# A gated feed-forward layer on one Trainium2 core: one pair of up-projection groups per layer computed token-major, with seven-product blocks

## The chip, the cores and the metric

The kernel runs on one core of one Trainium2 chip. The metric is the device time in microseconds of one execution. The engines are TensorE (PE, with its weight loads as PEld), VectorE (DVE), ScalarE (ACT), GpSimd (POOL) and SyncE (SP); SP and POOL issue the DMAs here.

## The reference

Two layers over 256 positions of width 2048, all in fp32. Layer 0 mixes positions with a gated MLP over blocks of 128, layer 1 with latent attention; each mixer is followed by a gated MLP with a causal width-3 convolution, which is what the change touches:

```
D_MODEL = 2048; SEQ = 256; DEPTH = 2; D_FF = 5504

def conv_ffn(x, w_up, conv_w, conv_b, w_down):
    h = x @ w_up                                    # (256, 2048) @ (2048, 11008)
    h = causal_depthwise_conv(h, conv_w) + conv_b   # width 3, along positions
    a, g = jnp.split(h, 2, axis=-1)
    return (jax.nn.silu(g) * a) @ w_down

x = layer_norm(ALPHA * x + mixer(x));  x = layer_norm(ALPHA * x + conv_ffn(x, ...))
```

## The kernel before

Every fp32 product is made of three products of rounded parts: high by high, low by high, high by low. A weight therefore has to be split: ACT casts its high part and DVE subtracts it to get the low part.

**The stream of weights.** All weights pass through one list of chunks of 1 MB (`Feed`, from line 73 on). SP loads a chunk into one of 3 "raw" slots, ACT and DVE split it (`wh` L127, `wl` L130) into two of 14 "big" slots, and the products read those. Splits are issued two chunks ahead of the use in the program; a scheduler then lays out the order on each engine, keeping each queue in order at run time. Chunk numbers stand in the names: `wl178` is the low part of chunk 178.

**Two forms of product.** In the feature-major form (`prod_a`) the weight block stands in the array and the activations stream: per group of 256 columns of the gate half and 256 of the value half, four chunks, four PSUM banks, 64 matmuls of 128x512 and 64 of 128x256. The result has features on partitions, as the convolution wants it. In the token-major form (`Banks`) the activation block stands and the weights stream, always 128x512; eight chunks serve four direct banks (`q3`, `p2`, `e`, `q4`) by `eight` with 24 matmuls a chunk. For a chunk marked "seven", `Feed._seven` (L133 on) also forms sums of the chunk's four 128x512 blocks (`ts`, then `th` and `tl`), and `Banks.seven` takes 21 matmuls in place of 24, using four more banks (`p1`, `q5`, `p7`, `p6`) and sums of the activations (`turn`, `combine`). `Banks.rest` (L448 on) combines the four extra banks on DVE. The token-major form with seven-chunks is used in the phases called v, u, wo, mo and dn.

**Up and down.** `ffn` runs up for groups 1 to 21 of four chunks each (group 0 is done earlier, with the mixer's end), all feature-major, seven-products nowhere. After each group `pair` runs twice: an ACT copy `lo` and a DVE sum `h` (L388, L390) join the halves of two banks, then the convolution (ACT L909, DVE L910 and L912), `silu` (ACT L926) and the product `act` (DVE L927). The names carry the pair's number: `h_0a15` is layer 0, value half, pair 15, that is, group 7. `act` tiles hold eight pairs each; from the fifth on (`act0_4`, `act0_5`) they live in "side" slots. Down (`dn`) follows, token-major in two halves, with every third or so chunk a "seven"; its banks take over those of the last up groups as the `h` rows free them.

**Parking.** Eight of the down chunks are split ahead, during up, and stored: `Feed.park` loads one by POOL (`praw`), splits it (`pwh`, `pwl`), makes the sums (four adds, L154) and splits those (`pth`, `ptl`); POOL stores the four results to DRAM (`keptwh`, `keptwl`, `keptth`, `kepttl`) and later fetches them (`fwh`, `fwl`, `fth`, `ftl`, L189). Six "side" slots hold all this. A chunk takes four steps, a layer 32; each step is taken by `next(jobs)` after chunks 1 and 2 of a group, from group 2 on. In layer 0 the parked chunks are 231 (used second in down), 236, 241 and so on to 266, the last that is parked. POOL's queue is in order, so a fetch that waits holds the ones behind it.

Of the kernel before, what the change touches and what calls it, by code (L numbers as in the profile page):

```python
# [8 lines left out]
F32 = mybir.dt.float32  # L9
# [6 lines left out]
P = 128  # L16
S = 256
# [35 lines left out]
U_SEVEN = [(2, 3)] + [(2, 3, 4)] * 4 + [(2, 3)]  # L53

MO_SEVEN = (1, 2)

T1, T2 = 6, 5
SLOTS = {"big": 14, "raw": 3, "side": 6}
# [15 lines left out]
def plan(n_k):  # L74

    return [[(int(t[:-1]), KINDS[t[-1]]) for t in line.split()] for line in PLAN[n_k]]
# [135 lines left out]
def trunk(ctx: ExitStack, tc: tile.TileContext, x, xT, gm_in, gm_wout, ffn_up, ffn_dn,  # L212
# [12 lines left out]
    def slot(shape, name, dt=F32, tag="big"):  # L225
        return big.tile(shape, dt, tag=tag, name=name, bufs=SLOTS[tag])

    def bank(name):
        return ps.tile([P, 512], F32, tag="bank", name=name)
# [27 lines left out]
    def back(w, n_k):  # L257

        for hf, units in enumerate(plan(n_k)):
            c = slice(hf * 1024, (hf + 1) * 1024)  # L260
            for u, kind in units:
                if 2 * u + 1 == n_k:
                    chunks.append((w[2 * u, :, c], 1024, kind))
                    continue
                if kind == "parked":
                    parked.append(len(chunks))
                chunks.append((w[2 * u : 2 * u + 2, :, c].rearrange("k p c -> p k c"), 2048, kind))

    back(gm_wout, NF_GM)
    chunks += [(ffn_up[0, i], 2048, "") for i in range(n_up)]  # L270
    back(ffn_dn[0], NF_FF)
    chunks += [(ml_q[i], 2048, "") for i in range(4)]
    chunks += [(ml_kv[i], 3 * KVR, "") for i in range(5)] + [(ml_kv[5, :, 0:KVR], KVR, "")]
    chunks += [(ml_b[i], 2048, "") for i in range(ml_b.shape[0])]
    chunks += [(ml_out[i], 2048, "seven" if i - 8 in MO_SEVEN else "") for i in range(ml_out.shape[0])]
    chunks += [(ffn_up[1, i], 2048, "") for i in range(n_up)]
    back(ffn_dn[1], NF_FF)


# [18 lines left out]
    def combine(name, o, k1, k2):  # L298


        t = tp.tile([P, 4, P], F32, tag="t2", name=f"xs{name}", bufs=T2)
        turn(t, k1, k2)
        o = o.rearrange("p (h s c) -> p h s c", h=2, s=4)
        nc.scalar.copy(o[:, 0], t)
        nc.vector.tensor_tensor(o[:, 1], t, o[:, 0].bitcast(F32), ALU.subtract)
        return [(o[:, 0, i], o[:, 1, i]) for i in (1, 2, 0, 3)]
# [556 lines left out]
    def park_all(until):  # L863

        for i in [i for i in parked if feed.used < i < until]:
            yield from feed.park(i)
            yield
# [48 lines left out]
    def ffn(layer, ln, acc, end, last):  # L916
        act = [None] * 6
        acts = Acts(act, f"dn{layer}", NF_FF)

        def pair(a, acc_a, acc_g):  # L920
            if act[a // 8] is None:
                act[a // 8] = slot([P, 8, S], f"act{layer}_{a // 8}", tag="side" if a // 8 > 3 else "big")
            ca = conv(layer, a, acc_a, f"{layer}a{a}")
            cg = conv(layer, NF_FF + a, acc_g, f"{layer}g{a}")
            s = tp.tile([P, S], F32, tag="t1", name=f"s{layer}_{a}", bufs=T1)
            nc.scalar.activation(s, cg, AF.Silu)  # L926
            nc.vector.tensor_tensor(act[a // 8][:, a % 8, :], s, ca, ALU.mult)  # L927

        hb, ht = [], [None, None]

        def after(b, step, acc):
            if step == 0:
                ht[b] = tp.tile([P, 512], F32, tag="t2", name=f"upt{layer}_{b}", bufs=T2)
                nc.scalar.copy(ht[b], acc)
                return
            if b == 0:
                hb.extend(bank(f"uph{layer}_{f}") for f in range(2))
            for f in range(4):
                o = (f % 2) * S + b * P
                nc.tensor.transpose(hb[f // 2][:, o : o + P], ht[b][:, f * P : (f + 1) * P], ident)  # L940

        boundary(ln, acc, end, f"upf{layer}_", after)
        xhl, old = ln.new, ln
        jobs = park_all(feed.used + 2 * n_up)
        for gi in range(1, 22):
            nt, nk = (4, 4) if gi < 21 else (2, 8)
            acc = [bank(f"up{layer}_{gi}_{f}") for f in range(nt)]
            for c in range(KD // nk):
                hi, lo = feed.next()
                prod_a(acc, xhl, range(nk * c, nk * c + nk), hi, lo)  # L950
                if gi > 1 and c in (1, 2) and gi + c > 3:
                    next(jobs, None)
                if (gi, c) in FIRST:
                    acts.make(*plan(NF_FF)[0][FIRST.index((gi, c))])
                if gi == 1 and c == 0:
                    after(1, 1, None)
                    for f in range(2):
                        pair(f, hb[0][:, f * S : (f + 1) * S], hb[1][:, f * S : (f + 1) * S])
            for f in range(nt // 2):
                pair(2 * gi + f, acc[f], acc[nt // 2 + f])  # L960
            if 1 < gi < 6:
                old.restore(gi - 2)
            if gi in (4, 6):
                old.park(gi // 2 - 2)
        ln = Norm(2 * layer + 1, {}, old.put_away, last)
        return (ln, *down(NF_FF, act, f"dn{layer}", ln, acts, 4 if last else SKEW))
# [406 lines left out]
```

## Time and profile before

| | |
|---|---|
| median of 3 runs | 2464.81 us (2464.58 to 2466.5) |
| the profiled execution's own time | 2465.45 us |
| its span | 2463.7 us |
| granted TensorE clock | 1.000 |
| DMA | 611.94 MB, mean 248 GB/s |

The span is what the profiler saw from the first to the last instruction. In the rows shown below, busy times are microseconds; "x" counts instructions; a group's row gives busy time and mean nanoseconds of one, then the idle time just before them and what ended it. In a row of the order in time the first number is the start, the second the length. Layer 0's group 8 starts at 972.1 us and its up projection ends at 1272.2 us; layer 1's up ends at 2231.8 us.

### The profile page before, as it was taken

To read this page: it belongs to the slowest core of one execution; us is meant where nothing else is said; L and a number is where in the kernel's file an instruction comes from. 1 tells how busy PE (TensorE), PEld (TensorE's weight loads), DVE (VectorE), ACT (ScalarE), POOL (GpSimd) and SP (SyncE) were. 2 spreads that over 40 slices of the span, in tenths; PEclk is the share of its full clock that TensorE was granted. 3 is DMA by queue.
4 is the path that set the end of the run, shared out by engine and by line. 5 is a ranking of instruction groups with operands and counts; after the bars stand their busy time and mean duration, and the time that the engine had idled before them with its cause. 6 is when DMAs were issued, how large, how long until landed. Compare 5 with 4: busy or idle time off the path is not lost. (4 is left out here: it accounts for less than half of the span.)

```text
span 2463.7 us, 32505 instructions
## 1 busy us (share of the span) xinstructions
PE 2456.6 (100%) x12488; PEld 2091.5 (85%) x12488; DVE 2070.3 (84%) x2762; ACT 1464.1 (59%) x1972; POOL 104.2 (4%) x202
## 2 busy tenths in 40 slices
PE   9999999999999999999999999999999999999999
PEld 7888888888888888888888888988888888888887
DVE  7999999989897788787777997868798787878798
ACT  6666665566565666556655566665665665555453
POOL 0000000000000000000000000000000000000000
PEclk9999999999999999999999999999999999999999
DMA  7555666656665778777868885543588787867885
GB/s 291 202 208 205 227 202 204 205 188 205 222 208 202 235 283 330 287 283 293 324 216 319 301 303 186 184 163 123 211 281 303 267 310 298 300 265 271 303 323 204
DMA packets 116428, 611.94 MB, mean 248 GB/s; under 512 B 10648, under 2 KB 10912, under 8 KB 75184
## 3 DMA queue, kind: packets, MB, share of 16 engines
q1 hardware_dynamic: 90128, 462.47, 52.9%
q0 software_dynamic: 26144, 147.39, 15.9%
q8 instruction: 98, 1.61, 0.3%
q14 instruction: 58, 0.48, 0.1%
HBM read 544.75 MB, written 65.06 MB: 248 GB/s over the span
## 5 line engine op out<-in xcount | busy, mean ns | idle before, releaser
L130 DVE TENSOR_TENSOR wl<-raw,wh 128x1024 fp32r<-128x1024 f32 (+4 forms) x643 | 956.4, 1502 | 164.2 <-ACT wh L127 120.6
L127 ACT CAST wh<-raw 128x1024 fp32r<-128x1024 f32 (+4 forms) x643 | 808.0, 1279 | 357.1 <-PE up L232 86.9
L232 PE MATMUL up<-xhl,wh 128*128 128x512 f32 x2624 | 611.4, 390 | 0.0
L232 PEld LDWEIGHTS up<-xhl,wh 128*128 128x128 f32 x2624 | 487.7, 188 | 97.5
L232 PEld LDWEIGHTS up<-xhl,wl 128*128 128x128 f32 x2624 | 325.8, 192 | 6.4
L232 PE MATMUL up<-xhl,wl 128*128 128x256 f32 x2624 | 328.1, 283 | 0.0
L127 ACT CAST th<-ts 128x1536 fp32r<-128x1536 f32 (+1 forms) x142 | 146.6, 1051 | 112.0 <-DVE ts L137 83.0
L232 PE MATMUL ub<-wh,xhl 128*128 128x512 f32 x576 | 179.7, 393 | 0.3 <-DVE u0w L454 0.3
L130 DVE TENSOR_TENSOR tl<-ts,th 128x1536 fp32r<-128x1536 f32 (+1 forms) x142 | 167.7, 1218 | 10.4 <-ACT th L127 3.4
L232 PEld LDWEIGHTS ub<-wh,xhl 128*128 128x128 f32 x576 | 108.1, 188 | 24.9 <-issue 1.9
L232 PE MATMUL ub<-wl,xhl 128*128 128x512 f32 x288 | 112.2, 390 | 0.0
L137 DVE TENSOR_TENSOR ts<-ts,raw 128x512 f32<-128x512 f32 x142 | 97.4, 686 | 1.5
L137 DVE TENSOR_TENSOR ts<-raw 128x1024 f32<-128x1024 f32 x71 | 86.5, 1219 | 7.3 <-PE ub L232 3.8
L232 PE MATMUL v_q<-wh,xhl 128*128 128x512 f32 x224 | 70.6, 391 | 0.4 <-ACT wh L127 0.4
L232 PEld LDWEIGHTS ub<-wl,xhl 128*128 128x128 f32 x288 | 54.1, 188 | 11.3
L232 PE MATMUL v_p<-wh,xhl 128*128 128x512 f32 x192 | 59.9, 389 | 0.0
L232 PEld LDWEIGHTS v_q<-wh,xhl 128*128 128x128 f32 x224 | 42.0, 188 | 10.1 <-ACT wh L127 1.5
L390 DVE TENSOR_TENSOR h_1a<-up,lo_1a 128x256 f32<-128x256 f32 x41 | 17.2, 419 | 33.0 <-ACT lo_1a L388 32.8
L390 DVE TENSOR_TENSOR h_0a<-up,lo_0a 128x256 f32<-128x256 f32 x41 | 17.2, 419 | 32.5 <-ACT lo_0a L388 32.5
L154 DVE TENSOR_TENSOR praw<-praw 128x512 f32<-128x512 f32 x64 | 43.9, 686 | 0.6
L726 ACT ACTIVATE lny<-lnt,lncol 128x128 f32<-128x128 f32 x96 | 36.3, 467 | 13.1 <-PE lnt L722 13.0
L232 PE MATMUL v_q<-wl,xhl 128*128 128x512 f32 x112 | 43.8, 391 | 0.1
(1885 smaller groups left out, 4418.6 us busy)
## 6 DMA issues: line engine op xcount, KB each, us to landing
raw<-in_ffn_up_dram SPq DMA_DIRECT2D x172, 1024.0 KB, 7.1
raw<-in_gm_in_dram SPq DMA_DIRECT2D x93, 1024.0 KB, 5.3
raw<-in_ffn_dn_dram SPq DMA_DIRECT2D x68, 1024.0 KB, 7.0
raw<-in_gm_wout_dram SPq DMA_DIRECT2D x48, 1024.0 KB, 5.2
praw<-in_ffn_dn_dram POOLq DMA_DIRECT2D x16, 1024.0 KB, 13.9
keptth<-pth POOLq DMA_DIRECT2D x16, 1024.0 KB, 8.1
kepttl<-ptl POOLq DMA_DIRECT2D x16, 1024.0 KB, 8.9
fth<-keptth POOLq DMA_DIRECT2D x16, 1024.0 KB, 9.6
```

What stands on the lines that cost most here:

```text
L127: cast = self.nc.scalar.copy(hi, raw)
L130: self.nc.vector.tensor_tensor(lo, raw, hi.bitcast(F32), ALU.subtract)
L137: add = lambda o, a, b: self.nc.vector.tensor_tensor(o, a, b, ALU.add)
L154: add = lambda o, a, b: pin(nc.vector.tensor_tensor(o, a, b, ALU.add))
L232: recent[0] = nc.tensor.matmul(o, l, r, start=start, stop=stop, skip_group_check=True)
L390: nc.vector.tensor_tensor(h, acc[:, 0:S], lo, ALU.add)
L726: nc.scalar.activation(y[:, j], t[:, j * P : (j + 1) * P], AF.Identity, bias=lncol[:, o : o + 1], scale=lncol[:, g : g + 1])
```

## The change

Groups 8 and 9 of each layer are taken together as one token-major pair of eight chunks, in the order 0, 2, 1, 3, 5, 4, 6, 7 of blocks of k; blocks 2, 3, 4 and 6 are "seven" chunks. What this needs:

- `sum_acts` makes the sums of the layer's input for those four blocks, during groups 5 and 6 (`xs`; the first room is two side slots, the later ones big slots);
- `token_group` runs the eight chunks and combines the banks (its four direct adds are L987 of the new file);
- `turn_group` turns the result to feature-major with 16 transposes of 128x128 after the first chunk of group 10, and `gate_group` runs the four pairs after its chunks 1 and 2, the convolution reading the transposed banks in PSUM directly;
- parking takes no step in group 7, one in the token pair and one in group 10, in place of two in each of groups 7 to 10; all later steps keep two per group, so the last four of the 32 steps are taken in groups 19 to 21 instead of 16 to 18.

```diff
+UP_TOKEN = (8,)
+UP_PAIRS = (0, 2, 1, 3, 5, 4, 6, 7)
+UP_SEVEN = (2, 3, 4, 6)
...
+            for p in UP_PAIRS:
+                i = 4 * gi + p // 2
+                w = ffn_up[layer, i : i + 5 : 4, :, p % 2 * 1024 : p % 2 * 1024 + 1024].rearrange("f p c -> p f c")
+                chunks.append((w, 2048, "seven" if p in UP_SEVEN else "wide"))
...
+        def sum_acts(p):
+
+            if len(sums) % 2 == 0:
+                rooms.append(slot([P, 2, 8 * P], f"xs{layer}_{p}", F32R, "side" if len(rooms) < 2 else "big"))
+            t = xhl[p // 2][:, 2 * (p % 2) : 2 * (p % 2) + 2]
+            raw = tp.tile([P, 2, S], F32, tag="t2", name=f"xr{layer}_{p}", bufs=T2)
+            nc.vector.tensor_tensor(raw, t[:, :, 0:S].bitcast(F32), t[:, :, S : 2 * S].bitcast(F32), ALU.add)
+            sums[p] = combine(f"{layer}_{p}", rooms[-1][:, len(sums) % 2, :], raw[:, 0], raw[:, 1])
+
+        def token_group(gi):
+
+            acc = Banks(f"upt{layer}_{gi}", DIRECT + OWN)
+            for c, p in enumerate(UP_PAIRS):
+                a = [[x_parts(xhl, 2 * p + j, b) for j in range(2)] for b in range(2)]
+                got = feed.next()
+                if c == 0:
+                    next(jobs, None)
+                if p in UP_SEVEN:
+                    acc.seven(a, sums[p], *got, turned=512, across=True)
+                    if p == [q for q in UP_PAIRS if q in UP_SEVEN][-1]:
+                        rest = acc.rest()
+                else:
+                    acc.eight(a, *got, across=True)
+            for n, t in zip(DIRECT, rest):
+                nc.vector.tensor_tensor(t, acc.acc[n], t, ALU.add)
+            turning.append((gi, rest, [bank(f"upr{layer}_{gi}_{i}") for i in range(4)]))
+
+        def turn_group():
+
+            gi, rest, t = turning[0]
+            for i, r in enumerate(rest):
+                b, f = i // 2, i % 2
+                for j in range(4):
+                    o = (j % 2) * S + b * P
+                    nc.tensor.transpose(t[2 * f + j // 2][:, o : o + P], r[:, j * P : (j + 1) * P], ident)
+
+        def gate_group(f):
+
+            gi, rest, t = turning[0]
+            for j in range(2):
+                c = slice(j * S, (j + 1) * S)
+                pair(2 * (gi + f) + j, t[2 * f][:, c], t[2 * f + 1][:, c])
+            if f == 1:
+                turning.pop()
+
         for gi in range(1, 22):
+            if gi - 1 in UP_TOKEN:
+                continue
+            if gi in UP_TOKEN:
+                token_group(gi)
+                continue
...
-                if gi > 1 and c in (1, 2) and gi + c > 3:
+                if gi > 1 and gi + 1 not in UP_TOKEN and c in ((3,) if gi - 2 in UP_TOKEN else (1, 2)) and gi + c > 3:
                     next(jobs, None)
...
+                if turning and c == 0:
+                    turn_group()
+                if turning and c in (1, 2):
+                    gate_group(c - 1)
+                if gi in (5, 6) and c % 2 and len(sums) < len(UP_SEVEN):
+                    sum_acts(UP_SEVEN[len(sums)])
```

What this does to the order of instructions, at three places of layer 0 (layer 1 is alike). Rows give the line, the operation, output, inputs and shape; line numbers of the changed file are up to 16 higher.

**The token pair.** On DVE, behind `h_0a14` (the first of group 7's sums), down to `h_0a15`, before:

```order
L130 TENSOR_TENSOR wl179_7637<-raw179_7520,wh179_7636 128x1024
L169 TENSOR_TENSOR ptl241_7677<-praw241_7296,pth241_7676 128x2048
L910 SCALAR_TENSOR_TENSOR c_0a14_7558<-h_0a14_7556,cst_176,c_0a14_7558 128x255
L390 TENSOR_TENSOR h_0g14_7564<-up0_7_2_7380,lo_0g14_7562 128x256
L912 SCALAR_TENSOR_TENSOR c_0a14_7558<-h_0a14_7556,cst_176,c_0a14_7558 128x254
L130 TENSOR_TENSOR wl180_7685<-raw180_7602,wh180_7684 128x1024
L910 SCALAR_TENSOR_TENSOR c_0g14_7566<-h_0g14_7564,cst_176,c_0g14_7566 128x255
L130 TENSOR_TENSOR wl180_7685<-raw180_7602,wh180_7684 128x1024
L912 SCALAR_TENSOR_TENSOR c_0g14_7566<-h_0g14_7564,cst_176,c_0g14_7566 128x254
L927 TENSOR_TENSOR act0_1_6893<-s0_14_7570,c_0a14_7558 128x256
L390 TENSOR_TENSOR h_0a15_7575<-up0_7_1_7379,lo_0a15_7573 128x256
```

and now:

```order
L172 TENSOR_TENSOR pwl241_7639<-praw241_7325,pwh241_7638 128x1536
L926 SCALAR_TENSOR_TENSOR c_0a14_7590<-h_0a14_7588,cst_176,c_0a14_7590 128x255
L406 TENSOR_TENSOR h_0g14_7596<-up0_7_2_7418,lo_0g14_7594 128x256
L928 SCALAR_TENSOR_TENSOR c_0a14_7590<-h_0a14_7588,cst_176,c_0a14_7590 128x254
L140 TENSOR_TENSOR ts179_7670<-raw179_7552 128x1024
L926 SCALAR_TENSOR_TENSOR c_0g14_7598<-h_0g14_7596,cst_176,c_0g14_7598 128x255
L140 TENSOR_TENSOR ts179_7670<-ts179_7670,raw179_7552 128x512
L928 SCALAR_TENSOR_TENSOR c_0g14_7598<-h_0g14_7596,cst_176,c_0g14_7598 128x254
L133 TENSOR_TENSOR wl179_7672<-raw179_7552,wh179_7671 128x1536
L140 TENSOR_TENSOR ts179_7670<-ts179_7670,raw179_7552 128x512
L943 TENSOR_TENSOR act0_1_6893<-s0_14_7602,c_0a14_7590 128x256
L406 TENSOR_TENSOR h_0a15_7607<-up0_7_1_7417,lo_0a15_7605 128x256
```

The plain splits of chunks 180 and 181 have left this run, and the heavier work on the seven-chunk 179 stands in it, with `pwl241` in place of `ptl241`. On PE, in the third chunk of the token pair (178) now:

```order
L235 MATMUL upt0_8_p2_7625<-wh178_7632,xhl1_0_5782 128x512 x2
L235 MATMUL upt0_8_p2_7625<-wl178_7633,xhl1_0_5782 128x512
L235 MATMUL upt0_8_p2_7625<-wh178_7632,xhl1_0_5782 128x512 x2
L235 MATMUL upt0_8_p2_7625<-wl178_7633,xhl1_0_5782 128x512
L235 MATMUL upt0_8_e_7626<-wh178_7632,xhl1_0_5782 128x512 x2
L235 MATMUL upt0_8_p7_7630<-th177_7541,xs0_2_7034 128x512 x2
L235 MATMUL upt0_8_p7_7630<-tl177_7542,xs0_2_7034 128x512
L235 MATMUL upt0_8_e_7626<-wl178_7633,xhl1_0_5782 128x512
L235 MATMUL upt0_8_e_7626<-wh178_7632,xhl1_0_5782 128x512 x2
L235 MATMUL upt0_8_p6_7631<-th177_7541,xs0_2_7034 128x512 x2
L235 MATMUL upt0_8_p6_7631<-tl177_7542,xs0_2_7034 128x512
```

The products `p7` and `p6` of the seven-chunk 177 stand behind those for `q3` and `p2` and inside those for `e` of chunk 178, not at the end of 177. Before, PE ran here the feature-major products of group 8.

**The start of down.** On PE, in its second chunk (231, fetched) and third (232), before:

```order
L232 MATMUL dn00_q4_10459<-fth231_10246,dn01px_10184 128x512 x2
L232 MATMUL dn00_q4_10459<-ftl231_10248,dn01px_10184 128x512
L232 MATMUL dn00_q5_10461<-fth231_10246,dn01px_10184 128x512 x2
L232 MATMUL dn00_q5_10461<-ftl231_10248,dn01px_10184 128x512
L232 MATMUL dn00_p7_10462<-fth231_10246,dn01px_10184 128x512 x2
L232 MATMUL dn00_p7_10462<-ftl231_10248,dn01px_10184 128x512
L232 MATMUL dn00_p6_10463<-fth231_10246,dn01px_10184 128x512 x2
L232 MATMUL dn00_p6_10463<-ftl231_10248,dn01px_10184 128x512
L232 MATMUL dn00_q3_10456<-wh232_10464,dn00wx_10019 128x512 x2
L232 MATMUL dn00_q3_10456<-wl232_10465,dn00wx_10019 128x512
L232 MATMUL dn00_q3_10456<-wh232_10464,dn00wx_10019 128x512 x2
L232 MATMUL dn00_q3_10456<-wl232_10465,dn00wx_10019 128x512
```

and now:

```order
L235 MATMUL dn00_q5_10449<-fth231_10222,dn01px_10152 128x512 x2
L235 MATMUL dn00_q5_10449<-ftl231_10224,dn01px_10152 128x512
L235 MATMUL dn00_q3_10444<-wh232_10452,dn00wx_9985 128x512 x2
L235 MATMUL dn00_q3_10444<-wl232_10453,dn00wx_9985 128x512
L235 MATMUL dn00_q3_10444<-wh232_10452,dn00wx_9985 128x512 x2
L235 MATMUL dn00_q3_10444<-wl232_10453,dn00wx_9985 128x512
L235 MATMUL dn00_p2_10445<-wh232_10452,dn00wx_9985 128x512 x2
L235 MATMUL dn00_p2_10445<-wl232_10453,dn00wx_9985 128x512
L235 MATMUL dn00_p7_10450<-fth231_10222,dn01px_10152 128x512 x2
L235 MATMUL dn00_p7_10450<-ftl231_10224,dn01px_10152 128x512
L235 MATMUL dn00_p2_10445<-wh232_10452,dn00wx_9985 128x512 x2
L235 MATMUL dn00_p2_10445<-wl232_10453,dn00wx_9985 128x512
```

`p7` of chunk 231 has moved behind nine matmuls of chunk 232 (and `p6`, further down, behind thirteen). On DVE at the same place, before:

```order
L927 TENSOR_TENSOR act0_5_10322<-s0_41_10358,c_0a41_10346 128x256
L390 TENSOR_TENSOR h_0a42_10437<-up0_21_0_10361,lo_0a42_10435 128x256
L490 TENSOR_TENSOR dn03sx_10494<-act0_0_6104,dn03sx_10494 128x512
L137 TENSOR_TENSOR ts233_10504<-ts233_10504,raw233_10401 128x512
L910 SCALAR_TENSOR_TENSOR c_0a42_10439<-h_0a42_10437,cst_176,c_0a42_10439 128x255
L390 TENSOR_TENSOR h_0g42_10445<-up0_21_1_10362,lo_0g42_10443 128x256
L912 SCALAR_TENSOR_TENSOR c_0a42_10439<-h_0a42_10437,cst_176,c_0a42_10439 128x254
L130 TENSOR_TENSOR wl233_10506<-raw233_10401,wh233_10505 128x1536
L910 SCALAR_TENSOR_TENSOR c_0g42_10447<-h_0g42_10445,cst_176,c_0g42_10447 128x255
L137 TENSOR_TENSOR ts233_10504<-ts233_10504,raw233_10401 128x512
L912 SCALAR_TENSOR_TENSOR c_0g42_10447<-h_0g42_10445,cst_176,c_0g42_10447 128x254
L130 TENSOR_TENSOR tl233_10508<-ts233_10504,th233_10507 128x1536
```

and now:

```order
L928 SCALAR_TENSOR_TENSOR c_0g41_10334<-h_0g41_10332,cst_176,c_0g41_10334 128x254
L943 TENSOR_TENSOR act0_5_10302<-s0_40_10319,c_0a40_10307 128x256
L140 TENSOR_TENSOR ts233_10492<-ts233_10492,raw233_10381 128x512
L943 TENSOR_TENSOR act0_5_10302<-s0_41_10338,c_0a41_10326 128x256
L133 TENSOR_TENSOR tl233_10496<-ts233_10492,th233_10495 128x1536
L406 TENSOR_TENSOR h_0a42_10425<-up0_21_0_10341,lo_0a42_10423 128x256
L133 TENSOR_TENSOR tl233_10496<-ts233_10492,th233_10495 128x512
L312 TENSOR_TENSOR dn06pt_10598<-act0_1_6893,dn06pt_10598 128x128
L926 SCALAR_TENSOR_TENSOR c_0a42_10427<-h_0a42_10425,cst_176,c_0a42_10427 128x255
L406 TENSOR_TENSOR h_0g42_10433<-up0_21_1_10342,lo_0g42_10431 128x256
```

The first writing of `act0_5`, for pair 40, stood far ahead of this run before and stands in its middle now, ahead of pair 41's, `tl233` and `h_0a42`; `ptl266` follows three rows later. That first writing now waits for PE's last read of `fwl231`, whose side slot it takes over.

**The last parked chunk.** POOL's queue of DMAs around chunk 266's stores and the first two fetches, before:

```order
L159 DMA keptwh266_9599<-pwh266_9595 128x1536
L159 DMA keptwl266_9601<-pwl266_9596 128x1536
L159 DMA keptth266_9813<-pth266_9809 128x2048
L159 DMA kepttl266_9815<-ptl266_9810 128x2048
L189 DMA fwh231_10242<-keptwh231_6585 128x1536
L189 DMA fwl231_10244<-keptwl231_6587 128x1536
L189 DMA fth231_10246<-keptth231_6807 128x2048
L189 DMA ftl231_10248<-kepttl231_6809 128x2048
L189 DMA fwh236_10520<-keptwh236_7030 128x1536
L189 DMA fwl236_10522<-keptwl236_7032 128x1536
L189 DMA fth236_10524<-keptth236_7252 128x2048
L189 DMA ftl236_10526<-kepttl236_7254 128x2048
```

and now:

```order
L162 DMA keptwh266_10206<-pwh266_10202 128x1536
L192 DMA fwh231_10218<-keptwh231_6585 128x1536
L162 DMA keptwl266_10208<-pwl266_10203 128x1536
L192 DMA fwl231_10220<-keptwl231_6587 128x1536
L192 DMA fth231_10222<-keptth231_6807 128x2048
L192 DMA ftl231_10224<-kepttl231_6809 128x2048
L162 DMA keptth266_10419<-pth266_10415 128x2048
L192 DMA fwh236_10508<-keptwh236_7030 128x1536
L162 DMA kepttl266_10421<-ptl266_10416 128x2048
L192 DMA fwl236_10510<-keptwl236_7032 128x1536
L192 DMA fth236_10512<-keptth236_7271 128x2048
L192 DMA ftl236_10514<-kepttl236_7273 128x2048
```

The fetch of chunk 231 now stands between the stores of 266's parts and those of its sums, and the store `kepttl266` stands between pieces of the fetch of 236.

More of the change, by code (lines that the diff above doesn't have):

```diff
@@ L267, in back, with up @@
                 chunks.append((w[2 * u : 2 * u + 2, :, c].rearrange("k p c -> p k c"), 2048, kind))
+    def up(layer):
+        for gi in range(22):
+            if gi - 1 in UP_TOKEN:
+                continue
+            if gi not in UP_TOKEN:
+                chunks.extend((ffn_up[layer, i], 2048, "") for i in range(4 * gi, min(4 * gi + 4, n_up)))
+                continue
[3 more added lines that the diff above has]
+                chunks.append((w, 2048, "seven" if p in UP_SEVEN else "wide"))
     back(gm_wout, NF_GM)
-    chunks += [(ffn_up[0, i], 2048, "") for i in range(n_up)]
+    up(0)
     back(ffn_dn[0], NF_FF)
@@ L275, in trunk @@
     chunks += [(ml_out[i], 2048, "seven" if i - 8 in MO_SEVEN else "") for i in range(ml_out.shape[0])]
-    chunks += [(ffn_up[1, i], 2048, "") for i in range(n_up)]
+    up(1)
     back(ffn_dn[1], NF_FF)
@@ L944, in ffn @@
         jobs = park_all(feed.used + 2 * n_up)
-        for gi in range(1, 22):
+        sums, rooms, turning = {}, [], []
+        def sum_acts(p):
[35 more added lines that the diff above has]
+                turning.pop()
+        for gi in range(1, 22):
+            if gi - 1 in UP_TOKEN:
+                continue
+            if gi in UP_TOKEN:
+                token_group(gi)
+                continue
             nt, nk = (4, 4) if gi < 21 else (2, 8)
```

## The prediction

> **What bounds the kernel now.** I read the page first (busy shares, then the chain of work that ended last), then the stretch-by-stretch table of busy times, then the groups of instructions with shapes kept apart, and last the order in time of PE, DVE and POOL at the two places that the change touches.
>
> ```profile
> span 2463.7 us, 32505 instructions
> PE 2456.6 (100%) x12488; PEld 2091.5 (85%) x12488; DVE 2070.3 (84%) x2762; ACT 1464.1 (59%) x1972; POOL 104.2 (4%) x202
> 1730.98 5.44 PE mo_q L232 x24
> 1781.87 450.10 PE up L232 x2592
> ```
>
> PE is busy 2456.6 of 2463.7 us. The second pair of rows is from the chain: start, length, what. Layer 1's up projection is one uninterrupted piece of 2592 matmuls, so whatever is taken from PE there shortens the run, and whatever makes PE wait there lengthens it. A group of up is 128 matmuls, half of them 128x512 and half 128x256: 450.10 / 2592 x 128 = 22.23 us, two groups 44.45. The mo_q piece holds 128x512 alone: 5.44 / 24 = 0.2267 us each.
>
> ```profile
> core 0: us, PE busy (x) PEld busy (x) DVE busy (x) ACT busy (x) POOL busy (x), PEclk, DMA share, GB/s
> 92.00:133.00 41.00, 41.00 (x183) 33.96 (x182) 39.81 (x38) 27.48 (x34) 0.00 (x0) 1.00 0.57 205
> 949.90:972.10 22.20, 22.20 (x129) 19.67 (x129) 18.61 (x27) 14.21 (x22) 1.09 (x2) 1.00 0.84 311
> 972.10:994.30 22.20, 22.20 (x130) 19.67 (x129) 14.61 (x21) 10.81 (x16) 1.77 (x3) 1.00 0.81 308
> 502.40:504.40 2.00, 2.00 (x19) 1.92 (x17) 1.94 (x3) 1.91 (x3) 0.00 (x0) 1.00 0.54 106
> ```
>
> The first stretch is a token-major group of the v phase with four seven-product chunks: the very form that two up groups are to take. PE has no gap in it, but DVE is at 39.81 of 41.00. The next two are groups 7 and 8 of layer 0's up, where DVE has 3.6 and 7.6 us to spare. The granted clock is 1.00 in all of them.
>
> **The change part by part.**
>
> *PE.* Removed per layer: 44.45 us. Added: four chunks of 24 and four of 21 matmuls, 180 x 0.2267 = 40.81 us, and 16 transposes.
>
> ```profile
> 502.48 1.91 PE L860 MATMUL ub<-ident,v 128*128 128x128 f32 x16
> L860 PE MATMUL ub<-ident,v 128*128 128x128 f32 x96 | 11.4, 273 | 0.0
> ```
>
> The first row is sixteen such transposes back to back. With the last one's 0.273 us taken off, their starts stand (1.91 - 0.27) / 15 = 0.109 us apart; 16 x 0.109 = 1.75. So 42.56 against 44.45: **1.9 us less per layer, 3.8 in all.** That is the whole gain; nothing else in the change takes work from the engine that sets the end. By the Trainium skill (TensorE: Matmul & The Clock Gate, Part 4: PE-mode transpose) a transpose costs about 275 ns in a kernel and does not count as activity for the clock. Its 275 agrees with the 273 as a duration, while the starts lie 0.109 apart and the stretch from 502.40 shows clock 1.00, so the sum keeps 1.75; with the page's figure it would be 4.4, and the gain negative.
>
> *DVE in the token group.* Prices, mean ns of one in the second number after the bar:
>
> ```profile
> L130 DVE TENSOR_TENSOR wl<-raw,wh 128x2048 fp32r<-128x2048 f32 x140 | 319.0, 2288 | 75.7 <-ACT wh L127 57.4 <-PE dn_q L232 13.8 <-issue 2.1
> L130 DVE TENSOR_TENSOR wl<-raw,wh 128x1536 fp32r<-128x1536 f32 x71 | 124.4, 1752 | 2.7 <-PE v_q L232 2.5 <-ACT wh L127 0.2
> L130 DVE TENSOR_TENSOR tl<-ts,th 128x1536 fp32r<-128x1536 f32 x71 | 124.4, 1753 | 10.4 <-ACT th L127 3.4 <-PE dn_p L232 3.4 <-PE v_p L232 1.9
> L130 DVE TENSOR_TENSOR tl<-ts,th 128x512 fp32r<-128x512 f32 x71 | 48.6, 684 | 0.0
> L137 DVE TENSOR_TENSOR ts<-raw 128x1024 f32<-128x1024 f32 x71 | 86.5, 1219 | 7.3 <-PE ub L232 3.8 <-DMA raw<-in_gm_in_dram 1.6 <-PE wo_q L232 0.7
> L137 DVE TENSOR_TENSOR ts<-ts,raw 128x512 f32<-128x512 f32 x142 | 97.4, 686 | 1.5
> L390 DVE TENSOR_TENSOR h_0a<-up,lo_0a 128x256 f32<-128x256 f32 x41 | 17.2, 419 | 32.5 <-ACT lo_0a L388 32.5
> L910 DVE SCALAR_TENSOR_TENSOR c_0a<-h_0a,cst,c_0a 128x255 f32<-128x255 f32 x41 | 19.7, 479 | 9.0 <-ACT c_0a L909 8.9
> L927 DVE TENSOR_TENSOR act<-s,c_0a 128x256 f32<-128x256 f32 x43 | 18.1, 422 | 12.1 <-ACT s L926 12.1
> ```
>
> A seven chunk costs 1.22 + 2 x 0.69 + 1.75 + 1.75 + 0.68 = 6.8 us on DVE for 21 x 0.2267 = 4.76 on PE; a wide one 2.29 for 5.44. Four of each: 36.3. The combining (four adds) and the four adds of direct banks, 128x512 each: 8 x 0.69 = 5.5. Two pairs of group 7 spill over, each two h, four conv steps (all at the 479 of L910) and one product: 2 x 3.2 = 6.3. One pwl of the parked chunk, a 128x1536 subtraction: 1.75. Together **49.9 us beside 40.8 of PE.** The missing 9.1 must come out of DVE's lead.
>
> ```profile
> 965.49 3.73 DVE L130 TENSOR_TENSOR wl<-raw,wh 128x1024 fp32r<-128x1024 f32 x3
> 1273.13 0.28 DVE L293 TENSOR_TENSOR dn03st<-act 128x128 f32<-128x128 f32 x1
> ```
>
> The first row (start, length) is the two halves of chunk 178 and the first half of 179, done by 969.2. At 5.56 us a chunk from 972.1, PE reads 178 at 983.2 and 179 at 988.8, so DVE leads by 14 to 20 us here. Leaving parking out of group 7 takes four of the 0.69 sums and later steps from DVE there; the sums of x in groups 5 and 6 put 10 us on it (four times two 128x512 steps at 0.69 and four 128x128 ones at the 0.28 of the second row, 2.5 together), which the same lead swallows. The lead thus covers 9.1 on the whole, but not at every point: DVE is in order, and the two banks that token chunk 177's last products p7 and p6 need are freed by h_0a15 and h_0g15, which stand behind a run of splits. From the start of the group, h_0a14 begins at about 0.9; the rows from it to h_0a15 add up to 0.42 + 1.75 + 0.48 + 0.42 + 0.48 + 1.22 + 0.48 + 0.69 + 0.48 + 1.75 + 0.69 + 0.42 + 0.42 = 9.7, so 10.6 without a wait, and 12 to 13 with the waits for ACT between them. PE reaches p7 after 24 + 15 + 12 + 2 = 53 matmuls (it has been moved behind part of 178), at 12.0, and p6 at 13.4. The later points of the group have 0.2 to 1 us of room by the same adding. I take **0.2 us a layer, bounds 0 and 1.5.** ACT, at 27.48 of 41.00 in the v stretch, is no bound.
>
> *The end of parking.* Of the 32 steps of a layer, the last four come three groups later, 3 x 22.23 = 66.7 us.
>
> ```profile
> 1181.30 0.56 POOL L159 DMA_DIRECT2D keptwh<-pwh  x1 [18.20 <-ACT pwh L168]
> 1184.20 0.53 POOL L159 DMA_DIRECT2D keptwl<-pwl  x1 [2.34 <-DVE pwl L169]
> 1203.70 0.53 POOL L159 DMA_DIRECT2D keptth<-pth  x1 [18.97 <-ACT pth L168]
> 1212.10 0.54 POOL L189 DMA_DIRECT2D ftl<-kepttl  x1 [3.65 <-DMA keptth<-pth]
> q0 software_dynamic: 864, 5.77, 36.3%
> kepttl<-ptl POOLq DMA_DIRECT2D x1, 1024.0 KB, 8.8
> ftl<-kepttl POOLq DMA_DIRECT2D x1, 1024.0 KB, 22.5
> ftl<-kepttl POOLq DMA_DIRECT2D x1, 1024.0 KB, 14.2
> DMA to landing us min/median/max: 6.9/9.6/22.1
> ```
>
> The first four rows are POOL's issues for the last parked chunk (266) and the first fetched one (231); then, from 1200 to 1240, POOL's bytes, and times to landing (the 14.2 from 1270 to 1300, of the next fetched chunk, 236); the last row is of all sixteen fth. The fetch of 231 (four pieces) ended at 1212.10 + 22.5 = 1234.6: 5.77 MB in 30.9 us after 1203.70, 187 GB/s. In the changed kernel keptwh266 goes out at 1181.30 + 66.7 = 1248.0, and the two stores and four fetches that follow (5.24 MB) end at 1276 by that rate; if ftl231, issued near 1260, again takes 22.5, at 1282.5. The stores of 266's sums wait longer still, for a side slot that only the reading of chunk 231 frees:
>
> ```profile
> 1279.48 0.39 PE L232 MATMUL dn_p<-fwl,dn01px 128*128 128x512 f32 x1
> 1280.16 0.39 PE L232 MATMUL dn_q<-ftl,dn01px 128*128 128x512 f32 x1
> 1281.07 0.62 PE L232 MATMUL dn_p<-fth,dn01px 128*128 128x512 f32 x2
> 1269.14 0.42 DVE L927 TENSOR_TENSOR act<-s,c_0a 128x256 f32<-128x256 f32 x1
> 1306.00 0.39 PE L232 MATMUL dn_q<-ftl,dn06px 128*128 128x512 f32 x1
> ```
>
> These are times of before; the changed kernel stands 1.9 earlier here throughout. ftl231 is needed at 1280.2: late by 0 to 2.3, I take 0. The product act0_5 (1269.14 now) takes such a slot too, and will wait for the fwl read at 1279.48, hence to 1279.8. Behind it on DVE stand a sum, a second product, tl233 and h_0a42: 0.42 + 0.69 + 0.42 + 1.75 + 0.42 = 3.7, so h_0a42, which frees the bank of p7, ends near 1283.3 with the slight overlap of successive rows. p7 starts at 1281.07 now; in the new order nine matmuls of chunk 232 stand ahead of it, 9 x 0.2267 = 2.04, so 1283.1. Those nine are the cover; without it about 3 us would be lost. I take 0.1, bounds 0 and 0.5.
>
> Then ptl266 (2.3) on DVE, so kepttl266 goes out near 1288.0, lands after 8.8 at 1296.8, and only then may ftl236, queued in order behind it on POOL, go. With the median fetch of 9.6 it lands at 1306.4 against a need of 1306.0; with the least, 6.9, at 1303.7; with 14.2, at 1311. I take 0.4, bounds 0 and 5. By the Trainium skill (DMA: Bandwidth & Descriptors, Anatomy of one DMA — SWDGE (gpsimd) path) a DMA takes about 2.0 us plus bytes / 436e3, an estimate of 4.4 us for 1 MB; both fetches would then be in time. The 8.8 and 22.5 beside other traffic say otherwise, so the measurement decides.
>
> *Sum.* 2465.45 (profiled execution; span 2463.7 and 1.75 around it) - 3.8 + 2 x (0.2 + 0.1 + 0.4) = 2463.05. The median of the runs is 0.64 below that execution: **2462.4.**
>
> **The rivals.**
>
> *The parked fetch comes late (slower).* Place: start of down, both layers. Price: 5 us where ftl236 lands at 1311; -3.8 + 10 gives 2471.0. It decides from 4.4 us a layer (2 x 4.4 - 3.8 = 5.0, past 0.2%). For it: the 22.5; against it: fewer fetches stand beside ftl236 than beside the 22.5 one. Chance 0.15.
>
> *DVE becomes the bound of the token group.* If a third of the 9.1 is not covered, 3 us a layer: 2464.81 - 3.8 + 6 = 2467.0; with all of it, 2479.2. For it: 39.81 of 41.00 in the v stretch, without the pairs and pwl that come on top here. Against it: the lead of 14 to 20. Chance 0.15.
>
> *Transposes at their duration.* If PE cannot overlap them, 16 x 0.273 = 4.4 in place of 1.75 adds 5.2 to the forecast: 2467.6. The sixteen in 1.91 us speak against it. Chance 0.04.
>
> *No net change,* the stalls eating just the gain: 2464.8, chance 0.03. That the change doesn't take its matmuls away cannot be; per layer 256 go and 196 come.
>
> **How the numbers follow.** The forecast has 0.60; its own range is 2461.0 (no stall) to 2465.0 (2 us a layer). 0.03 is left for a time below 2459.9, for which I see no source. 0.2% is 4.9 us, about what a measurement of this kernel can tell from no change; the gain alone cannot reach it. Slower by more than that: two thirds of the first rival and a third of the second, 0.15. Faster 0.03, within 0.82. The range runs from 2460.4, a little below no stall for the spread of the runs, to 2469.0, which leaves out those tails.
>
> **What would show it.** PE busy falls by 3.8, and the chain of layer 1's up keeps one piece with shorter length: the gain is right. Idle time of PE before upt p7 or p6, released by h_0a15 or h_0g15, beyond 0.5 a layer: the DVE ledger is wrong. Idle time before dn_q or dn_p in the first seven chunks of down, released by ftl: the first rival; released by h_0a42: the cover of nine matmuls falls short. Wrong altogether if PE waits for raw chunks or for xs in groups 5 to 10, since I cost loads and sums of x at nothing.

## The result, and the profile after

The changed kernel takes **2474.09 us** (median; 2473.66 to 2474.82) against 2464.66 for the one before in the same runs: a ratio of 1.0038, 95% interval 1.0026 to 1.0049. It is 9.4 us slower, where 2462.4 was forecast.

From the page of the changed kernel:

```profile
span 2472.9 us, 32347 instructions
PE 2456.8 (99%) x12368; PEld 2084.8 (84%) x12368; DVE 2120.4 (86%) x2834; ACT 1475.5 (60%) x1966; POOL 104.2 (4%) x202
```

PE has 120 instructions fewer, as meant, yet no less busy time, and 9.2 us more of span. The first place to look is therefore not the work but the waits. What PE waited for in the changed kernel, most costly first (total us, times, longest):

```profile
PE dn_p L235 <- DVE h_1a L406: 3.7, 1, 3.7
PE dn_p L235 <- DVE h_0a L406: 3.4, 1, 3.4
PE dn_q L235 <- DMA ftl<-kepttl: 2.1, 1, 2.1
PE warm L235 <- POOL idle L299: 1.3, 1, 1.3
```

The first three are new, and all lie in the first chunks of down, the phase behind the one that was changed. The token pair itself did what it was to do. Stretch by stretch (columns as in the prediction), its eight chunks in layer 0, then two stretches behind the new waits; below, from the chain, its transposes in layer 1:

```profile
971.18:1012.20 41.02, 41.02 (x182) 33.65 (x180) 38.81 (x44) 25.23 (x28) 1.09 (x2) 1.00 0.62 215
...
1309.20:1313.20 4.00, 4.00 (x11) 3.14 (x12) 2.88 (x4) 1.68 (x1) 0.00 (x0) 0.57 1.08 420
2250.20:2255.50 5.30, 5.26 (x16) 4.20 (x17) 4.64 (x8) 4.13 (x6) 0.53 (x1) 0.68 0.98 368
```

```profile
1983.82 1.75 PE upr L997 x16
...
2227.07 12.71 DMA raw<-in_ffn_dn_dram
...
2250.24 1.71 PE dn_p L235 x6
```

The eight chunks took 41.02 us and the sixteen transposes 1.75: 42.77 where two feature-major groups took 44.45, so 1.7 us were gained in layer 0. In layer 1 the eight chunks took 41.34, and 1.4 were gained. The second and third stretches show something that no term of the prediction held: the granted clock fell to 0.57 and 0.68. In 4.00 us PE began 11 matmuls, where 4.00 / 0.2267 would be 17.6; the missing 6.6 are worth 1.5 us, and in the third stretch 23.4 - 16 = 7.4 are worth 1.7. And the chain names a transfer that I had not on my list: 12.7 us of loading a **plain** down chunk (raw), not a parked one.

How that leads to the wait, in layer 0 of the changed kernel (start, length; in brackets the idle time before and what ended it):

```profile
1268.32 1.91 ACT L130 CAST wh<-raw 128x2048 fp32r<-128x2048 f32 x1 [3.61 <-DMA raw<-in_ffn_dn_dram]
...
1270.26 2.29 DVE L133 TENSOR_TENSOR wl<-raw,wh 128x2048 fp32r<-128x2048 f32 x1 [3.34 <-ACT wh L130]
...
1283.39 0.41 DVE L406 TENSOR_TENSOR h_0a<-up,lo_0a 128x256 f32<-128x256 f32 x1
...
1283.95 0.70 PE L235 MATMUL dn_p<-fth,dn01px 128*128 128x512 f32 x2 [3.36 <-DVE h_0a L406]
...
1309.20 0.51 PE L235 MATMUL dn_q<-ftl,dn06px 128*128 128x512 f32 x1 [2.07 <-DMA ftl<-kepttl]
```

The same two DVE instructions in the kernel before:

```profile
1269.81 2.28 DVE L130 TENSOR_TENSOR wl<-raw,wh 128x2048 fp32r<-128x2048 f32 x1
...
1276.43 0.42 DVE L390 TENSOR_TENSOR h_0a<-up,lo_0a 128x256 f32<-128x256 f32 x1
```

Both `wl` rows split chunk 232. ACT sat idle for its raw data, DVE for ACT, and from there DVE ran without a gap to `h_0a42`, which PE's `p7` was waiting for. The transfers issued from 1243 to 1268 us, changed kernel (median time to landing at the end of the row):

```profile
raw<-in_ffn_dn_dram SPq DMA_DIRECT2D x4, 1024.0 KB, 11.9
...
fth<-keptth POOLq DMA_DIRECT2D x1, 1024.0 KB, 13.8
ftl<-kepttl POOLq DMA_DIRECT2D x1, 1024.0 KB, 10.8
...
keptwl<-pwl POOLq DMA_DIRECT2D x1, 768.0 KB, 9.8
fwl<-keptwl POOLq DMA_DIRECT2D x1, 768.0 KB, 12.7
```

and before:

```profile
raw<-in_ffn_dn_dram SPq DMA_DIRECT2D x3, 1024.0 KB, 5.2
```

Before, only SP's loads were issued here and took 5.2 us; now POOL's stores of chunk 266 and its fetch of 231 run beside them and they take 11.9. From 1256 to 1268 us the DMA engines are now busy throughout, where a third of their time was free before (the last two numbers are their busy share and GB/s; first now, then before):

```profile
1256.00:1268.00 12.00, 12.00 (x70) 10.57 (x69) 9.25 (x13) 4.56 (x7) 0.53 (x1) 1.00 1.04 401
...
1256.00:1268.00 12.00, 12.00 (x74) 10.73 (x73) 8.61 (x12) 6.73 (x10) 0.00 (x0) 1.00 0.65 217
```

That gave the theory: **the postponed end of parking crowds the DMA engines just when down's first chunks are loaded.** Its rival is the new order on DVE alone (the waits for side slots ahead of `h_0a42`); another is the token pair and its sums of x.

### The profile page after: what moved, and what is told of

Same layout as the page of the kernel before. It is cut to its first block, busy times and chain, and to the rows that moved or that the text cites. A ratio compares the mean times of both kernels' runs of the same rounds, so it can differ in the third digit from the quotient of the medians.

```text
span 2472.9 us, 32347 instructions
## 1 busy us (share of the span) xinstructions
PE 2456.8 (99%) x12368; PEld 2084.8 (84%) x12368; DVE 2120.4 (86%) x2834; ACT 1475.5 (60%) x1966; POOL 104.2 (4%) x202
## 5 line engine op out<-in xcount | busy, mean ns | idle before, releaser
L235 PE MATMUL up<-xhl,wh 128*128 128x512 f32 x2368 | 552.1, 390 | 0.0
L235 PEld LDWEIGHTS up<-xhl,wh 128*128 128x128 f32 x2368 | 439.8, 188 | 88.2
L235 PEld LDWEIGHTS up<-xhl,wl 128*128 128x128 f32 x2368 | 294.1, 192 | 5.8
L235 PE MATMUL up<-xhl,wl 128*128 128x256 f32 x2368 | 296.6, 283 | 0.0
L130 ACT CAST th<-ts 128x1536 fp32r<-128x1536 f32 (+1 forms) x158 | 163.3, 1051 | 119.8 <-DVE ts L140 96.9
L133 DVE TENSOR_TENSOR tl<-ts,th 128x1536 fp32r<-128x1536 f32 (+1 forms) x158 | 186.5, 1216 | 11.0 <-ACT th L130 3.9
L140 DVE TENSOR_TENSOR ts<-ts,raw 128x512 f32<-128x512 f32 x158 | 108.2, 685 | 1.6
L140 DVE TENSOR_TENSOR ts<-raw 128x1024 f32<-128x1024 f32 x79 | 96.1, 1217 | 12.1 <-DMA raw<-in_ffn_dn_dram 6.2
L742 ACT ACTIVATE lny<-lnt,lncol 128x128 f32<-128x128 f32 x96 | 36.3, 467 | 13.2 <-PE lnt L738 13.1
L235 PE MATMUL mo<-wh,oT 128*128 128x512 f32 x128 | 42.8, 412 | 0.0
L235 PE MATMUL upf<-wh,xhl 128*128 128x512 f32 x128 | 42.3, 403 | 0.3 <-ACT xhl L745 0.2
## 6 DMA issues: line engine op xcount, KB each, us to landing
praw<-in_ffn_dn_dram POOLq DMA_DIRECT2D x16, 1024.0 KB, 14.6
```

Of the source, the lines that this page charges most:

```text
L130: cast = self.nc.scalar.copy(hi, raw)
L133: self.nc.vector.tensor_tensor(lo, raw, hi.bitcast(F32), ALU.subtract)
L140: add = lambda o, a, b: self.nc.vector.tensor_tensor(o, a, b, ALU.add)
L235: recent[0] = nc.tensor.matmul(o, l, r, start=start, stop=stop, skip_group_check=True)
L742: nc.scalar.activation(y[:, j], t[:, j * P : (j + 1) * P], AF.Identity, bias=lncol[:, o : o + 1], scale=lncol[:, g : g + 1])
```

## The experiments

Each kernel ran beside the kernel before on the same chip; medians are compared with that one's, 2464.75 in the first four and 2464.79 in the last three. The numbers behind a time are its ratio to that median and the 95% interval of the ratio. The diffs are shortened, and the remarks behind "#" are added here.

**e1, parking caught up at three steps a group.**

```diff
-c in ((3,) if gi - 2 in UP_TOKEN else (1, 2))
+c in ((3,) if gi - 2 in UP_TOKEN else (1, 2, 3) if 11 <= gi <= 16 else (1, 2))
```

> The changed kernel, but the six parking steps left out around the token pair are caught up: three steps instead of two in groups 11 to 16, so that parking ends in group 18 as before the change. Theory (the lateness of the last parked chunk costs the time): PE's waits in the first chunks of down go (3.4 + 2.1 us in layer 0, 3.7 in layer 1, and the slow matmuls behind them), some 13 us, and about 2461 us is left, 3.5 below the kernel before. Rival (the token pair itself, its sums of x or its load on DVE cost the time): it stays above 2465.

Measured: 2490.42 us, 1.0104 (1.009 to 1.0117), the slowest of all. The waits at down are gone, but others have come. What PE waited for in all, and the first rows of what ACT and DVE waited for from 1030 to 1220 us:

```profile
PE up L235 <- DVE wl L133: 16.0, 11, 5.0
```

```profile
ACT pwh L171 <- DMA praw<-in_ffn_dn_dram: 36.4, 5, 10.6
...
DVE pwl L172 <- ACT pwh L171: 20.4, 3, 11.3
DVE c_0g L926 <- ACT c_0g L925: 18.5, 5, 10.1
```

Three steps a group put a parked chunk's first cast (`pwh`) one or two up chunks behind its load instead of three. The load takes 15.9 us here (the median of five; 14.6 in the changed kernel), ACT waits for it in its queue, and the group work behind it on ACT and DVE waits too. The forecast of 2461 us missed; the time is on the rival's side (above 2465), but not for the rival's reason, since the waits lie where parking catches up. So this run says nothing against the theory at down, but the catching up has to keep the distance of load and cast. It was done so in e10.

**e2, the pause without the token pair.** The kernel before with only the steps of the pause left out, made from the changed file by taking the token pair and its sums away:

```diff
-UP_TOKEN = (8,)
+UP_TOKEN = ()
...
-if gi > 1 and gi + 1 not in UP_TOKEN and c in ((3,) if gi - 2 in UP_TOKEN else (1, 2)) and gi + c > 3:
+if gi > 1 and c in {7: (), 8: (1,), 9: (), 10: (3,)}.get(gi, (1, 2)) and gi + c > 3:
...
-if gi in (5, 6) and c % 2 and len(sums) < len(UP_SEVEN):
+if UP_TOKEN and gi in (5, 6) and c % 2 and len(sums) < len(UP_SEVEN):
```

> The kernel before, all groups feature-major, with only the pause of the change: no parking step in groups 7 and 9, one each in 8 and 10. Theory: the start of down shows the same waits on h_0a42 and ftl as the changed kernel, about 13 us in all, so about 2477 us. Rival (the token pair costs the time): 2465, no wait at the start of down.

Measured: 2477.62 us, 1.0051 (1.0038 to 1.0065), 12.9 us more than before. Its waits of PE:

```profile
PE dn_p L235 <- DVE h_1a L406: 3.8, 1, 3.8
PE dn_p L235 <- DVE h_0a L406: 3.7, 1, 3.7
...
PE dn_q L235 <- DVE h_0g L406: 0.4, 1, 0.4
```

All groups are feature-major here, and the loss is there in full: 12.9 us, beside the 9.4 of the changed kernel and the 3.1 that its token pairs gained. The waits shown are 7.9 of it; the rest is slow clock, as PE is busy for 5.8 us more than before with the same 12488 matmuls. The token pair and its sums are cleared; the pause costs the time. The wait for `ftl` didn't come in this run, so this part of the forecast failed: it is the less certain part.

**e3, the token pair without the pause.**

```diff
-if c == 0:
+if c in (1, 2, 5, 6):
     next(jobs, None)
...
-gi + 1 not in UP_TOKEN and c in ((3,) if gi - 2 in UP_TOKEN else (1, 2))
+c in (1, 2)
```

> The changed kernel with parking as before the change: two steps in group 7, four in the token pair, two in group 10. Theory: nothing is late at down; DVE has some 9 us more to do in and ahead of the token pair, where its ledger was full, so PE waits there, by 1 to 5 us a layer: 2462 to 2470 us. If the pause was not needed at all: 2461.

Measured: 2468.95 us, 1.002 (1.0011 to 1.0029). No wait at down, but in and behind the token pair:

```profile
PE upt_p L235 <- DVE h_0a L406: 1.7, 1, 1.7
...
PE up L235 <- DVE upt_8d L472: 1.1, 2, 0.5
PE upt_q L235 <- DVE wl L133: 0.9, 2, 0.5
PE upt_p L235 <- DVE h_1a L406: 0.8, 1, 0.8
```

These are the points at which the prediction's ledger of DVE was full (`p7`, the splits, the combining). The eight chunks took 44.25 and 43.29 us in the two layers, 3.2 and 2.0 more than with the pause. So without the pause the pair loses what it gains; with it, the price is paid elsewhere.

**e7, late parking with fewer bytes.** Of chunk 266's four results (436 in layer 1) 256 columns are stored, and fetched back repeatedly; the order on every engine is that of the changed kernel.

```diff
+cols = 256 if i in (266, 436) else cols
 d = self.dram.tile([P, cols], F32, ...)
...                                         # and the fetch repeats these columns
```

> The changed kernel, every engine's order the same, but of each of the last parked chunk's four results only 256 columns are stored (and fetched back several times over), so that its part of the down product is not the reference's: 1.3 MB less on the DMA engines at 1249 to 1262 us and 1.8 MB less at 1283 to 1297. Theory (the late stores and the first fetch crowd the loads of down's first chunks, so ACT and DVE start late): chunk 230 lands some 3 us earlier, DVE's idle 3.3 us ahead of its split shrinks below 1.5, the wait for h_0a42 shrinks from 3.4 to 1.5 or less, the wait for ftl goes: 2461 to 2466 us. Rival (the order on DVE with its waits for side slots is enough by itself): the wait for h_0a42 stays at 3.4 and 3.7 us, only that for ftl goes, about 2470.

Measured: 2471.69 us, 1.0034 (1.0022 to 1.0047). The five executions spread from 2469.48 to 2477.42, and the profiled one is the fastest of them. In its layer 0, around the split of chunk 232 (which the expectation calls 230):

```profile
1268.13 1.91 ACT L130 CAST wh<-raw 128x2048 fp32r<-128x2048 f32 x1 [2.70 <-DMA raw<-in_ffn_dn_dram]
...
1270.08 2.29 DVE L133 TENSOR_TENSOR wl<-raw,wh 128x2048 fp32r<-128x2048 f32 x1 [2.42 <-ACT wh L130]
...
1283.77 0.70 PE L241 MATMUL dn_p<-fth,dn01px 128*128 128x512 f32 x2 [2.46 <-DVE h_0a L412]
```

Neither forecast fits: the wait is 2.46, where theory had 1.5 or less and the rival 3.4. Only the wait for `ftl` of chunk 236 went, as both had it. But beside the changed kernel's rows the pattern is plain: ACT's idle time fell by 0.9 (3.61 to 2.70), DVE's by 0.9 (3.34 to 2.42) and PE's wait by 0.9 (3.36 to 2.46). From the changed kernel to this one PE's wait follows the late load one for one; 1.3 MB less had only moved it that little.

**e8, most of the bytes gone.** As e7, and of each of chunk 231's four fetched pieces (401 in layer 1) only 512 columns, used for all its blocks.

```diff
+if i in (231, 401):
+    self.behind(self.nc.gpsimd.dma_start(t[:, 0:512], d[:, 0:512]))
+    t = Same(t)        # every block of 512 columns reads these
```

> As e7 (the last parked chunk's four results stored by 256 columns only), and of each of the first fetched chunk's four pieces only 512 columns are fetched and used for all its blocks: both chunks' parts of the down product are not the reference's. The order on PE, DVE, ACT and SP is that of the changed kernel; 3.9 of the 5.2 MB of POOL's transfers ahead of 1262 us are gone. Theory (two things add up: the order puts h_0a42 6.5 us later on DVE, which PE's cover of 4.2 + 2.0 us just takes, and the late load of down's chunks 230 and 232 adds 3.1, which shows in full): the loads take 5 to 6 us again, DVE's idle time ahead of the split of 232 is under 0.7, the waits for h_0a42 and h_1a42 are under 0.7 each, 2461 to 2464 us. Rival (the order alone): the waits stay at 2.5 us or more, 2467 or more.

Measured: 2464.7 us, 1.0001 (0.9992 to 1.0009). From the trace, the split of chunk 232 and `h_0a42` on DVE, and the loads from 1243 to 1268:

```profile
1266.77 2.29 DVE L142 TENSOR_TENSOR wl<-raw,wh 128x2048 fp32r<-128x2048 f32 x1
...
1279.88 0.42 DVE L424 TENSOR_TENSOR h_0a<-up,lo_0a 128x256 f32<-128x256 f32 x1
```

```profile
raw<-in_ffn_dn_dram SPq DMA_DIRECT2D x4, 1024.0 KB, 5.8
```

The loads are back to 5.8 us, DVE has no idle time ahead of the split, `h_0a42` starts 3.5 us earlier, and no wait for it stands among PE's waits any more, in either layer. The cover just holds: `h_0a42` ends at 1280.30 and `p7` starts at 1280.45. One wait of this kernel's own is left: its repeated fetch of 266 comes late.

```profile
PE dn_q L253 <- DMA ftl<-kepttl: 2.5, 1, 2.5
```

That one ends at 1454.4 us, is followed by half clock from 1455.2 to 1458.6, and is no part of the question; with it the median lies 0.7 above the forecast of 2461 to 2464. So with the changed order on PE, DVE and ACT (on POOL two neighbouring issues a layer changed places) but without the bytes, the loss at the start of down is gone.

**e12, traffic without the order.** The kernel before, with six copies of 1 MB that nothing uses:

```diff
+if (gi, c) in ((20, 2), (20, 3), (21, 0)):
+    for n in range(2):
+        d = dram.tile([P, 2048], F32, ...)
+        behind(nc.scalar.dma_start(d, hi.bitcast(F32)))
```

> The kernel before, with six copies of 1 MB from SBUF to DRAM (used by nothing) issued by ACT between chunks 20.2 and 21.0 of up, at some 1243 to 1262 us: traffic like that of the late parking, with h_0a42 in its old place on DVE. Theory (order and traffic have to come together): the loads of down's first chunks take 9 us or more instead of 5.2, yet PE waits less than 1 us for h_0a42 in each layer: 2465 to 2468 us. Rival (late loads alone cost the time): waits of 3 us or more a layer, 2471 or more.

Measured: 2466.17 us, 1.0005 (0.9996 to 1.0014). Transfers from 1243 to 1268, what DVE waited for from 1240 to 1290, and the start of `p7` on PE:

```profile
copy<-wh ACTq DMA_DIRECT2D x4, 1024.0 KB, 6.2
raw<-in_ffn_dn_dram SPq DMA_DIRECT2D x2, 1024.0 KB, 7.9
```

```profile
DVE wl L130 <- issue: 5.3, 1, 5.3
DVE wl L130 <- PE up L232: 4.8, 1, 4.8
```

```profile
1287.96 0.62 PE L232 MATMUL dn_p<-fth,dn01px 128*128 128x512 f32 x2
```

The loads were slowed less than expected (7.9 us; one of them 10.6), and DVE stood still mostly for another reason, twice for some 5 us (probably as the copies hold slots of the split weights; that is not shown). PE never waited for `h_0a42` and lost 0.8 us in all, to `wl`. But the run can't decide between theory and rival, because its edit moved PE's order at the start of down as well: `p7` starts 15.0 us behind the first product of down (1273.00), where it started 8.8 behind it before (1281.07 - 1272.23). In its old place it would have been due at 1281.8, while `h_0a42` ended at 1283.07. So no run shows late loads with the old order. What the old order would have borne is an estimate from the rows of before: `h_0a42` ended at 1276.85 and `p7` started at 1281.07, 4.2 us to spare, more than the 3.3 by which DVE was late.

**e10, caught up with the load kept three chunks ahead.**

```diff
+CATCH = {(11, 0): 2}                        # (group, chunk): steps
+for _n in range(5):                         # one parked chunk per 6 up chunks, not 8
+    for _d in ((0, 3, 4, 5) if _n else (3, 4, 5)):
+        CATCH[divmod(44 + 6 * _n + _d, 4)] = 1
...
+if gi > 10:
+    for _ in range(CATCH.get((gi, c), 0)):
+        next(jobs, None)
```

> The changed kernel with parking caught up in another way than in e1: from group 11 on one parked chunk per 6 up chunks instead of 8, its load always 3 chunks (16.7 us) ahead of its first cast as before the change, which the first catch-up broke; the last step is in group 18, as before the change. Theory: no wait at the start of down, none in up beyond the 0.2 to 0.5 us of the token pair: 2461 us (2460.5 to 2462.5), 3 to 4 below the kernel before. If DVE cannot take 6.8 us per 33 us beside group work, PE waits for wl in groups 11 to 18, and it ends above 2464.

Measured: **2462.06 us, 0.9988 (0.9979 to 0.9997)**, 2.7 us below the kernel before and 12 below the changed one: the fastest here. From its page and its waits of PE:

```profile
PE 2453.3 (100%) x12368; PEld 2083.4 (85%) x12368; DVE 2119.5 (86%) x2834; ACT 1476.9 (60%) x1966; POOL 104.2 (4%) x202
```

```profile
PE upt_p L241 <- DVE h_1a L412: 0.8, 1, 0.8
```

PE is busy for 3.3 us less than before (2456.6), and only one wait of 0.8 in layer 1's token pair is left of those that the change brought. The last piece of chunk 231's fetch is issued at 1214.15, where it was 1212.10 before, and down takes what it took before. From its first product to the next phase, in layer 0 and layer 1, that is 217.8 and 221.8 us before, 225.5 and 227.3 in the changed kernel, 225.3 and 228.2 in e2, and 217.8 and 221.7 in both e3 and e10. The mechanism holds in both directions: give the last parked chunk its old time, and the gain of the token pair appears. (The order at the start of down goes back with it, so this run doesn't part order and traffic; e8 does, for the traffic.)

## Why the prediction was wrong, point by point

- **The gain on PE: right.** 1.9 us a layer less 0.2 of stalls was forecast; 44.45 - 42.77 = 1.7 was measured in layer 0 and 1.4 in layer 1, stalls in it.
- **The ledger of DVE in the token pair: right.** The waits for `h_0a15` and its like were too short to stand among PE's waits in the changed kernel, and e3 shows that the points named were those on the edge. The rival "DVE becomes the bound" did not come; in e3 a part of it did.
- **Parking's issue times: nearly right.** keptwh266 went out at 1249.0 (forecast 1248.0 less 1.9, so 2.9 late); ftl231, needed at 1277.5, landed in time, at 1262.25 + 10.8.
- **The cover of nine matmuls at `p7`: the step that failed.** It was given 0.1 us, bounds 0 and 0.5, and cost 3.4 and 3.7. The order behind it was read rightly: e8, with that order and no crowding, has no such wait. But the sum let DVE arrive at `act0_5` in time to wait for its slot, and so put the loads of down's plain chunks at nothing, without a reason: its line "I cost loads and sums of x at nothing" is about groups 5 to 10. The wait for the slot never came: PE began the last read of fwl231 at 1276.80, and DVE reached `act0_5` only at 1280.45. The loads of down's plain chunks went from 5.2 to 11.9 us, DVE came 3.3 us late, and as the new order had used up the cover (h_0a42 ran 6.6 us behind the split of 232 before, 1276.43 - 1269.81, and 13.1 now), all of it showed. That the old order would have hidden it is an estimate (see e12). I had put the late parking's transfers beside each other and asked when they land; I had not asked what else lands beside them.
- **ftl236: mechanism right, size off.** 0.4 was taken, bounds 0 and 5. In layer 0 it was issued at 1297.5 and PE's wait for it ended at 1309.2, 11.7 later instead of the 9.6 taken, and PE waited 2.1. In layer 1 there was no such wait, nor in e2.
- **The clock: not in the sum at all.** Two of the three waits were followed by matmuls at about half speed, which cost 1.5 and 1.7 us.

The new losses add up: 3.4 + 3.7 + 2.1 of waits and 3.2 of slow clock are 12.4; less 1.7 and 1.4 gained, 9.3, where the span grew by 9.2. The first rival had the side and the place (parked transfers late at the start of down, 2471.0 us), but through a parked fetch; in fact most of it came through the plain loads and a DVE queue, so that its time is near 2474.1 is in good part luck. A rival for the loads, with 5.2 us set against what 5.2 MB of extra traffic would make of it, was missing.

## What to carry to other kernels

A background stream that pauses in one phase ends later in another: cost the place where it ends, with every transfer that it will run beside, and not only the place where it makes room. An order that just covers one wait has, by the estimate under e12, spent the slack that would have taken the next; when a reordering hides something "exactly", ask what else could be late on the engine behind it. When catching up, keep the distance between a load and the first instruction that waits for it in an in-order queue, or the cure costs more (e1) than the pause did.

## What the hardware showed that was not expected

In the changed kernel a wait of 2.1 us (1307.13 to 1309.20) was followed by half clock, and so was one of 3.7 (2246.52 to 2250.24), while the one of 3.4 (1280.59 to 1283.95) was not. The length of a wait doesn't tell, but its place does. The stretches of half clock start at 1309.56 and 2251.64 and last 3.41 us each, and their starts are 942.08 us apart, 276 times 3.413. In e2 they last twice 3.41, and their starts (1285.47 and 2251.44) are 283 times 3.413 apart. So the clock changes on a grid of 3.41 us in these traces. Here are the cells of that grid that hold the three waits, with the cells of half clock behind them:

```profile
1278.84:1282.25 3.41, 1.75 (x8) 1.13 (x6) 3.41 (x6) 2.43 (x3) 0.00 (x0) 1.00 0.01 5
1282.25:1285.67 3.42, 1.72 (x8) 1.45 (x9) 3.42 (x8) 3.20 (x8) 0.54 (x1) 1.00 0.84 237
1306.15:1309.56 3.41, 1.34 (x7) 0.80 (x6) 3.41 (x6) 1.99 (x2) 1.06 (x2) 1.00 1.03 413
1309.56:1312.97 3.41, 3.41 (x10) 2.64 (x9) 2.52 (x3) 1.45 (x1) 0.00 (x0) 0.50 1.06 413
...
2248.23:2251.64 3.41, 1.40 (x6) 1.21 (x7) 3.41 (x7) 3.19 (x7) 0.54 (x1) 1.00 0.74 217
2251.64:2255.05 3.41, 3.41 (x9) 2.63 (x9) 2.75 (x3) 2.25 (x3) 0.53 (x1) 0.50 0.99 390
```

The wait of 3.4 falls into two cells, and PE is idle (the cell less its busy time) for 1.7 us of each; the cells ahead of half clock have 2.1 and 2.0. The other traces agree, away from their two ends: cells at full clock with 1.95 us idle or more (e2 twice, e1, e8) are followed by half clock, cells with 1.60 or less are not. Between these lie four of 1.7 without it (the two above, one at 2244.81 in the changed kernel and one at 982.00 in e3) and one of 1.64, at 2137.39 in e1, with it. So about half a cell of idle time was enough here.

By the Trainium skill (TensorE: Matmul & The Clock Gate, Part 1: The HAM clock gate) the clock halves after an idle window of about 3.4 us that runs free of the kernel, and returns after as much busy time. The length of the window and the return behind a busy one agree with the rows above; that the whole window has to be idle does not, and here the measurement decides. So the wait of 2.1 us cost 1.5 us more than its length, the one of 3.7 cost 1.7 more (those of e2, with two cells of half clock, some 2.9), and the one of 3.4 nothing more, by where they fell on the grid. That fits the spread of one and the same program: e7's five executions had mean clocks from 1.000 (2469.48 us) to 0.997 (2477.42 us).
